# One order per engine for the whole of a hybrid encoder layer, with twenty-five instructions in other places

## The chip, the cores and the metric

The kernel runs on one core of a Trainium2 chip, in one launch. Its time is what the device takes for one execution, in microseconds (us); of a kernel run several times the median is given. The engines of the core are TensorE (PE in the profile: matmuls; PEld is its loading of weights), VectorE (DVE), ScalarE (ACT) and GpSimd (POOL); nearly all transfers are issued by SyncE (SP). Each engine takes its instructions one after the other in the order of the program, and waits at one whose inputs, or whose space for the output, are not ready.

## What is computed

One layer of an encoder, on 1024 rows of a new stream (the prompt) and 64 rows of a running one (the sample rows), 1024 wide:

```
z = x @ w_in, cut by columns into
  fox  (6 heads of 64): softmax(q k^T / 8 + c_t - c_s, causal) v,  c = cumsum(log f)
  sgu  (4 groups of 64): gelu(u) * (tril(w_s) @ layer_norm(gelu(v)) + b_s), chunks of 128
  sb   (6 heads of 64): stick-breaking weights in log space, strictly causal, times v
o = RMSNorm per head(concat) * g_mix
x = layer_norm(ALPHA * x + o @ w_out)
x = layer_norm(ALPHA * x + square(relu(x @ w_up)) @ w_down)       # 1024 -> 4096 -> 1024
```

The sample rows attend to 512 cached keys of their own as well. New keys, values and gates are outputs too. Everything is float32.

## The kernel before

A matmul of float32 accuracy is made from three passes in TensorE's faster format. Each operand is split into a high part, which ScalarE copies, and the rest, which VectorE or GpSimd subtracts (`split`, the subtraction is L182 throughout). So a tile that TensorE multiplies always comes from a pair of instructions on two engines.

**Attention** goes through three head pairs of fox and then three of stick-breaking. For each, keys and values of all rows are projected (L452, from `wkv` splits at L428), queries are projected, doubled by an exchange through a transfer (`qd`, L206, L602), and scores are made by blocks (`S`, L651). For fox VectorE takes maxima (`T` and `m`, L623), ScalarE exponentials; for stick-breaking VectorE scans (`sn`, L635). The weights are transposed on TensorE (`pt`, L699), split (`pth`, L667 and L182), multiplied with the values (`o`, L709 to L712), copied out (`osb`, L722), transposed again (`otp`, L730) and reduced (`ot`, L731). Beside the attention the output weights are brought in, scaled and put back to memory in parts (`rwo`, `swo`, `wo_dr`: L1074, L1081, L1082, L1085), and the spatial gate is computed. The output projection (`mx`, L335) and the layer norm follow.

**The border to the MLP** transposes the normed rows (L1293) and builds seven operand tiles `xo` per half of the rows by additions (L1313 to L1327) and splits (L1298, L1303, L182).

**The MLP** uses seven products for each two-by-two block (a Strassen scheme). Up (L1419, sixteen pairs `p`, each for two halves `s` of the rows of 288 and 256): the products go into PSUM banks `zA`, `zB`, `zC`, `zD`; ScalarE copies a zA into `sn` or `hh` (L1430), VectorE combines (L1433 to L1439), squares the positive part (L1451), makes sums (L1460 to L1463), and the result `hh` is stored to memory (`h_dr`, `h4_dr`, `h3_dr`, and `hs_dr` for the sample rows). Down (L1884, sixteen `g`, each with two `x`): rows `hx`, `awa`, `hr` of h are loaded and split, by way of a staging tile `st` in PSUM: ScalarE copies the high part (L1578), writes it to `st` (L1582), VectorE subtracts `st` from the rows (L1583). The weights `rd` are loaded (L1533), combined in place (L1551) and split (ScalarE L1357, then L182): tiles `wd` and `b12`. The products land in banks `A`, `B`, `D` and are added by VectorE to `acc` and, for the first tile, `awa` (L1849, L1851). A second layer norm ends the kernel (L1894, L1953 to L1997).

`st` takes its PSUM bank in turn from two, and one of these is the bank that `zD` of the first half uses as well.

**What sets the order.** The program is traced by a Python loop. From the start of attention to its end, four tables of letters and counts in `ORDER` fix the order of TensorE, ScalarE, VectorE and GpSimd: each instruction falls into a lane by the name of its output, each letter takes the next of a lane. After attention a scheduler places the instructions by its own costs, except inside blocks `with in_order(border)`, which tie each engine's instructions to the order in which the code writes them. SyncE has no table.

The diff touches `in_order`, two places in the function that traces the layer, and the tables.

## Time and profile before

| | us |
|---|---|
| median of three runs | 1377.58 |
| lowest and highest | 1376.11, 1380.68 |
| the profiled execution | 1378.24 |
| its span | 1376.2 |
| TensorE busy in it | 1317.1 |
| VectorE busy | 996.0 |
| ScalarE busy | 719.7 |
| GpSimd busy | 617.1 |

The mean granted clock of TensorE was 0.99. In the timeline a row has the start, the length of the busy time, the engine, the line, the operation, the output and its inputs by the program's names with the buffer numbers left out, the shapes, and a count where several alike were joined. What stands in brackets is the idle time of the engine ahead of the row and what ended it. In the table by stage each engine has its busy time, in the order PE, PEld, DVE, ACT, POOL, then the granted clock, the share of time that the transfer engines were busy, and GB/s.

### The profile page before, as it was taken

The numbers are of one execution on the slowest core, as the hardware profiler recorded it, in microseconds if no ns is written. First come the engines' busy times: TensorE is split into PE (matmuls) and PEld (weight loads), VectorE is DVE, ScalarE is ACT, GpSimd is POOL, SyncE is SP. The second block draws the span as 40 slices with busy tenths as digits, with TensorE's granted clock in tenths as the row PEclk, the third lists the DMA queues.
The fourth block names the chain that finished last, engine by engine and source line by source line (L and its number), as shares of the span: only waits on it lengthen the run. The fifth ranks groups of instructions, "written<-read, shape, count | busy, mean of one in ns | idle before, by whom it ended". The sixth has DMA issues, their size and how long they took to land.

```text
span 1376.2 us, 24318 instructions
## 1 busy us (share of the span) xinstructions
PE 1317.1 (96%) x8827; PEld 1200.1 (87%) x8827; DVE 996.0 (72%) x1797; ACT 719.7 (52%) x1561; POOL 617.1 (45%) x666
## 2 busy tenths in 40 slices
PE   7999999999989998999999999999999999999996
PEld 7898989999888997778899999999976787887774
DVE  4577666576888389678875877877677676767677
ACT  4366566566656376334523322322267676767665
POOL 3222222255675456657402221221176665655557
PEclk9999999999999999999999999999999999999999
DMA  7445565141303257432244435344567344434343
GB/s 227 108 118 143 163 189 145 52 100 43 103 13 76 63 185 252 140 115 70 77 153 135 144 119 171 131 131 162 176 219 277 123 146 142 142 119 159 99 136 131
DMA packets 158048, 185.64 MB, mean 135 GB/s; under 512 B 27740, under 2 KB 116124, under 8 KB 157928
## 3 DMA queue, kind: packets, MB, share of 16 engines
q1 hardware_dynamic: 155832, 183.01, 41.7%
q8 instruction: 70, 1.15, 0.4%
q10 hardware_dynamic: 2096, 1.07, 0.3%
q14 instruction: 50, 0.41, 0.1%
HBM read 117.65 MB, written 60.10 MB: 129 GB/s over the span
## 4 chain that ended last, share of the span: by engine, by line
PE 56%; DVE 14%; DMA 10%; ACT 8%; POOL 7%; issue 5%; SPq 0%; ACTq 0%; DVEq 0%; POOLq 0%
PE zA L1419 9%; PE zD L1419 6%; PE mx L335 5%; PE kvsb L452 5%; PE A L1884 5%; PE kvfox L452 3%; PE zB L1419 3%; DMA rwo<-w_out 3%; PE zC L1419 3%; DMA rd<-w_down 2%; PE D L1884 2%; POOL wd L182 2%; PE qsb L593 2%; DVE snsb L635 1%; POOL rd L1551 1%
## 5 line engine op out<-in xcount | busy, mean ns | idle before, releaser
L182 POOL TENSOR_TENSOR wa<-wr,wa 128x512 fp32r<-128x512 f32 x41 | 64.4, 1598 | 220.1 <-ACT wa L1357 202.5
L182 POOL TENSOR_TENSOR wd<-rd,wd 128x512 fp32r<-128x512 f32 x77 | 100.5, 1317 | 108.8 <-ACT wd L1357 104.3
L335 PE MATMUL mx<-xT,oTb 128*128 128x512 f32 (+1 forms) x416 | 105.1, 404 | 1.4 <-DVE oTb L182 1.3
L1419 PE MATMUL zD<-xo,ws 128*128 128x288 f32 (+1 forms) x720 | 97.5, 289 | 2.7 <-DVE h4a L1583 1.7
L1419 PE MATMUL zA<-xo,ws 128*128 128x288 f32 (+1 forms) x720 | 97.0, 289 | 0.0
L1419 PEld LDWEIGHTS zD<-xo,ws 128*128 128x128 f32 x720 | 93.4, 189 | 3.4 <-DVE h4a L1583 2.0
L335 PEld LDWEIGHTS mx<-xT,oTb 128*128 128x128 f32 (+1 forms) x416 | 76.0, 188 | 20.4 <-DVE oTb L182 2.2
L1551 POOL TENSOR_TENSOR rd<-rd 128x512 f32<-128x512 f32 x56 | 79.5, 1419 | 31.1 <-DVE b L182 28.8
L1419 PEld LDWEIGHTS zA<-xo,ws 128*128 128x128 f32 x720 | 93.4, 189 | 0.0
L452 PE MATMUL kvfox<-wkvfox,xT 128*128 128x256 f32 (+3 forms) x624 | 89.7, 292 | 3.1 <-ACT wkvfox L428 3.0
L452 PE MATMUL kvsb<-wkvsb,xT 128*128 128x256 f32 (+1 forms) x624 | 88.8, 287 | 0.4 <-ACT wkvsb L428 0.4
L637 POOL TENSOR_TENSOR sgsb<-sgsb,snsb 128x127 f32<-128x127 f32 (+7 forms) x48 | 59.6, 1244 | 65.9 <-DVE snsb L635 54.5
L1357 ACT ACTIVATE wd<-rd 128x512 fp32r<-128x512 f32 x105 | 63.5, 623 | 46.6 <-POOL rd L1551 23.6
L1884 PE MATMUL A<-wd,wd 128*128 128x512 f32 x312 | 83.4, 396 | 3.3 <-DVE acc L1851 2.3
L452 PEld LDWEIGHTS kvfox<-wkvfox,xT 128*128 128x128 f32 (+1 forms) x624 | 81.1, 191 | 4.4 <-ACT wkvfox L428 3.4
L635 DVE TENSOR_TENSOR_SCAN snsb<-snsb,one 128x128 f32<-128x128 f32 (+7 forms) x48 | 72.1, 1505 | 12.0 <-ACT snsb L634 10.9
L452 PEld LDWEIGHTS kvsb<-wkvsb,xT 128*128 128x128 f32 (+1 forms) x624 | 79.5, 187 | 0.8 <-ACT wkvsb L428 0.6
L1430 ACT ACTIVATE sn<-zA 128x256 f32<-128x256 f32 (+1 forms) x80 | 31.0, 390 | 85.2 <-PE zA L1419 74.9
L1884 PEld LDWEIGHTS A<-wd,wd 128*128 128x128 f32 x312 | 58.0, 188 | 19.5 <-DVE acc L1851 4.0
L1884 PE MATMUL A<-wd,h4a 128*128 128x512 f32 x240 | 64.5, 394 | 1.6 <-DVE awa L1851 0.8
L1640 ACT ACTIVATE ws<-wr 128x1024 fp32r<-128x1024 f32 x28 | 29.1, 1057 | 59.2 <-DVE wr L1369 59.2
L1884 PEld LDWEIGHTS A<-wd,h4a 128*128 128x128 f32 x240 | 44.6, 188 | 13.3 <-DVE awa L1851 1.2
(551 smaller groups left out, 3749.1 us busy)
## 6 DMA issues: line engine op xcount, KB each, us to landing
h_dr<-hh SPq DMA_DIRECT2D x30, 512.0 KB, 3.2
rd<-w_down SPq DMA_DIRECT2D x30, 512.0 KB, 4.5
wr<-w_up SPq DMA_DIRECT2D x13, 1024.0 KB, 5.5
hr<-h_dr SPq DMA_DIRECT2D x31, 384.0 KB, 4.4
h_dr<-hh SPq DMA_DIRECT2D x30, 384.0 KB, 3.6
raw<-w_in SPq DMA_DIRECT2D x44, 256.0 KB, 3.3
wo_dr<-swo SPq DMA_DIRECT2D x32, 256.0 KB, 2.3
xT<-wo_dr SPq DMA_DIRECT2D x8, 1024.0 KB, 7.0
```

Of the source, the lines that this page charges most:

```text
L182: eng.tensor_tensor(out, src, hi.bitcast(F32), op=ALU.subtract)
L335: nc.tensor.matmul(acc[0:m], oT[:, k, hx, 0:m], wo[k // 4][hw][:, k % 4, cs], start=(i == 0), stop=(i == len(seq) - 1))
L452: nc.tensor.matmul(acc[0:n, c0:c0 + n1 - n0], xT[k // 4][:, k % 4, c:c + n], wt[:, k, hw, n0:n1], start=(i == 0), stop=(i == len(seq) - 1))
L593: nc.tensor.matmul(acc[:, 0:w], wq[:, k, hw, :], xT[k // 4][:, k % 4, c:c + w], start=(i == 0), stop=(i == len(seq) - 1))
L635: nc.vector.tensor_tensor_scan(g[:, 0:n][:, ::-1], g[:, 0:n][:, ::-1], one.broadcast_to([P, n]), 1.0, op0=ALU.mult, op1=ALU.bypass)
L637: nc.gpsimd.tensor_tensor(s[:, 0:n - 1], s[:, 0:n - 1], g[:, 1:n], op=ALU.mult)
L1357: nc.scalar.activation(hi, raw, AF.Copy)
L1419: nc.tensor.matmul(z, w[:, hw, k], xop(s, bo, hx)[:, k, :], start=(new and k == 0 and j == 0), stop=(k == 3 and j == 2), skip_group_check= ...
L1430: nc.scalar.activation(c, z, AF.Copy)
L1551: eng.tensor_tensor(r[:, o], r[:, x], r[:, y], op=ALU.subtract)
L1640: nc.scalar.activation(ws[:, 0, q, c], src[:, q], AF.Copy)
L1884: nc.tensor.matmul(z, h[:, hx, q, o], wset[self.c % 2][q][:, hw, wb], start=((n in (0, 3) or n == 1 and self.c == 0) and q == 0 and j == 0 ...
```

## The change

The tables now hold numbers, one table an engine, and cover everything from the start of attention to the end of the program, MLP and border included. A word `n+k` means: n times, take the k-th of the instructions of this engine that are left, counted in the order of the trace. The order is laid down at the end of the trace, after everything has been written. `in_order` now ties SyncE's instructions alone, and the one use of it that was for TensorE alone is gone.

```diff
 ORDER = {}
-TICK = {"PE": {"kv": 0, "pt": 2, "sgm": 2, "mx": 1}, "ACT": {}, "DVE": {"T": 0, "sgvv": 0, "y": 0}, "POOL": {}}
-KIND = {
...
-}
 ORDER["PE"] = """
-8u e 8u 23e 24e' 8u k 8u k 14e 4u 2e' 10e 22e' 4u 8e k 4e 7u k 5u 12e 4u 14e' 2u 10e' 8e k 15e k e 14u 24e'
...
+9 8+23 55 +8 8+25 +8 14 4+34 2+10 45 4+1 7+13 1 +12 4+36 12 4+24 14 2+36 19 15+1 8 8+24 24 +8 8 8+1 9 8+1
...
     @contextmanager
-    def in_order(prev=None, only=None):
+    def in_order(prev=None):
...
         for i in traced[at:]:
-            if only is not None and i.engine != only:
+            if i.engine != nc.sync.engine:
                 continue
...
-        phase_1 = len(traced)
+        from_here = len(traced)
...
-        def lane_of(i, eng, code):
...
-        for eng, e in (("PE", nc.tensor), ("ACT", nc.scalar), ("DVE", nc.vector), ("POOL", nc.gpsimd)):
...
-            assert not any(lanes.values()), eng
-
...
-                    with in_order(border, nc.tensor.engine) if p == 2 else nullcontext():
+                    with nullcontext():
                         ch.product(i)
...
+    for eng, e in (("PE", nc.tensor), ("ACT", nc.scalar), ("DVE", nc.vector), ("POOL", nc.gpsimd)):
+        left = [i for i in traced[from_here:] if i.engine == e.engine]
+        prev = None
+        for word in ORDER[eng].split():
+            n, k = (int(x or d) for x, d in zip(re.match(r"(\d*)\+?(\d*)", word).groups(), (1, 0)))
+            for _ in range(n):
+                i = left.pop(k)
+                if prev is not None:
+                    tc.add_manual_dep(i, prev.name, mybir.DependencyInfo(
+                        mybir.DependencyClass.NoSync, mybir.DependencyReason.DATA), reason="order")
+                prev = i
+        assert not left, eng
```

Every engine has the same instructions as before. TensorE has them in the same order. On ScalarE and VectorE a dozen each stand elsewhere, on GpSimd one (L1953 of the sample rows' norm, now ahead of L1986), and on SyncE five places differ (in fox0 `raw2182_0` and `raw2182_1`, loads at L427, each pass a store of `swo7_0`; a load of cached keys, a load of `y4` and a load of `hr1_1` are the others). Line numbers are larger after the change: L1357, L1430, L1435, L1551, L1578, L1583 and L1851 become L1367, L1440, L1445, L1561, L1588, L1593 and L1861.

In attention: on VectorE `swo3_1` (L1082) goes behind `Tfox1_5_1` (L623), `swo7_0` behind `Tfox0_3_1`, `pthsb0_1_0_0` ahead of the second `qdsb0_3`, `otsb1_0_0` (L731) ahead of the scan of `snsb1_3_1`; on ScalarE `wqsb0` ahead of `Tfox0_3_0`, `osbfox0_0_0` ahead of `swo7_0`, `pthfox0_1_1_0` ahead of `swo7_1`, `qssb0` behind `osbsb0_0_1` and `pthsb0_1_0_1`. At the border to the MLP: on ScalarE one copy `xo13` goes behind `c123` (L1309) and one copy `xo14` ahead of `sn0_1` (L1430); on VectorE `hh1_0<-zD` goes ahead of `hh1_0<-zB`. The others lie at the border from up to down, at the start of the down products and in the last of them.

The first place is the border from up to down, where the last up products (`p` 15, half 0) meet the first splits for down. ScalarE before:

```order
L1430 ACTIVATE sn15_0_12435<-zA15_0_12437 128x288
L1357 ACTIVATE wd0_0_12451<-rd0_0_12254 128x512
L1357 ACTIVATE wd0_1_12452<-awa_12332 128x512
L1578 ACTIVATE h4a_12327<-h4a_12327 128x512
L1582 ACTIVATE st3_12472<-h4a_12327 128x512
```

ScalarE with the change:

```order
L1367 ACTIVATE wd0_0_12451<-rd0_0_12254 128x512
L1367 ACTIVATE wd0_1_12452<-awa_12332 128x512
L1588 ACTIVATE h4a_12327<-h4a_12327 128x512
L1440 ACTIVATE sn15_0_12435<-zA15_0_12437 128x288
L1592 ACTIVATE st3_12472<-h4a_12327 128x512
```

The copy of the product zA into `sn15_0` now comes after two weight copies and one copy of h. VectorE at the same place, before:

```order
L1435 TENSOR_TENSOR hh15_0_12436<-zB15_0_12457,sn15_0_12435 128x288
L1583 TENSOR_TENSOR h4a_12327<-h4a_12327,st3_12472 128x512
L1583 TENSOR_TENSOR h4a_12327<-h4a_12327,st4_12476 128x512
L1551 TENSOR_TENSOR rd0_0_12254<-rd0_0_12254 128x512
L1551 TENSOR_TENSOR awa_12332<-awa_12332 128x512
```

VectorE with the change:

```order
L1593 TENSOR_TENSOR h4a_12327<-h4a_12327,st3_12472 128x512
L1593 TENSOR_TENSOR h4a_12327<-h4a_12327,st4_12476 128x512
L1561 TENSOR_TENSOR rd0_0_12254<-rd0_0_12254 128x512
L1445 TENSOR_TENSOR hh15_0_12436<-zB15_0_12457,sn15_0_12435 128x288
L1561 TENSOR_TENSOR awa_12332<-awa_12332 128x512
```

The combination `hh15_0` of the product zB has moved behind both subtractions of h and one combination of weights. `st3` shares its bank with `zD15_0`.

Near the start of the down products VectorE moves three more: `wd0_1` by `st8` (L1583) goes behind the addition of `A0_0` to `awa`, and the addition of `A1_1` to `acc37` goes ahead of `h4b` by `st19` (L1583) and of the addition of `p11_1` to the same `acc37`. ScalarE takes one copy of `hr0_1` into `wd0_1` (L1578) before two weight copies (L1357).

The second place is in the last products, on ScalarE, ahead of the rows for the down product 13 (`hr13`, `hx`, `awa` are rows of h, `b12_0` is a weight tile made from `rd7_0`). Before:

```order
L1582 ACTIVATE st108_14998<-h4a_12327 128x512
L1578 ACTIVATE h4a_12327<-hx_12333 128x512
L1578 ACTIVATE h4a_12327<-awa_12332 128x512
L1578 ACTIVATE wd0_0_12451<-hr13_0_14899 128x384
L1578 ACTIVATE wd0_0_12451<-hr13_1_14901 128x384
L1357 ACTIVATE b12_0_12584<-rd7_0_14840 128x512
```

With the change:

```order
L1592 ACTIVATE st108_14998<-h4a_12327 128x512
L1367 ACTIVATE b12_0_12584<-rd7_0_14840 128x512
L1588 ACTIVATE h4a_12327<-hx_12333 128x512
L1588 ACTIVATE wd0_0_12451<-hr13_0_14899 128x384
L1588 ACTIVATE wd0_0_12451<-hr13_1_14901 128x384
L1588 ACTIVATE h4a_12327<-awa_12332 128x512
```

The weight copy `b12_0` has moved from behind four copies of h to ahead of them, and the copy from `awa` behind those from `hr13`. VectorE's addition of `ds6_1` (the sample rows' product) to `awa` goes ahead of one subtraction at the same time. A little earlier ScalarE takes a copy of `wd1_0` behind `st103`, `hr12_1` and the preload `B12_1` (L1872).

The third place is some fifteen microseconds later in the profile, on VectorE. Before:

```order
L1583 TENSOR_TENSOR h4b_12587<-awa_12332,st116_15169 128x512
L1851 TENSOR_TENSOR acc37_12748<-p113_1_15058,B13_1_15078 128x512
L182 TENSOR_TENSOR b12_1_12586<-rd7_1_15037,b12_1_12586 128x512
L1851 TENSOR_TENSOR acc26_12592<-acc26_12592,D13_0_15128 128x512
L1851 TENSOR_TENSOR acc37_12748<-acc37_12748,A13_1_15049 128x512
```

With the change:

```order
L1593 TENSOR_TENSOR h4b_12587<-awa_12332,st116_15169 128x512
L1861 TENSOR_TENSOR acc37_12748<-p113_1_15058,B13_1_15078 128x512
L1861 TENSOR_TENSOR acc26_12592<-acc26_12592,D13_0_15128 128x512
L215 TENSOR_TENSOR b12_1_12586<-rd7_1_15037,b12_1_12586 128x512
L1861 TENSOR_TENSOR acc37_12748<-acc37_12748,A13_1_15049 128x512
```

The addition of `D13_0` has passed the split of `b12_1`.

More of the change, by code (lines that the diff above doesn't have):

```diff
@@ L49 @@
 ORDER = {}
-TICK = {"PE": {"kv": 0, "pt": 2, "sgm": 2, "mx": 1}, "ACT": {}, "DVE": {"T": 0, "sgvv": 0, "y": 0}, "POOL": {}}
-KIND = {
-    "PE": "a:S b:Ss0 c:Ss1 d:ftp e:kv f:mx g:o h:op i:os j:otp k:pk l:pkc m:pt n:ptn o:pts p:q q:sgm "
-           "r:sgu s:sgv t:wstp u:xtp",
-    "ACT": "a:T b:f c:g d:gsv e:kc f:kn g:kp h:kvs i:oTb j:osb k:pth l:pths m:ptnn n:qd o:qs p:qsz "
-           "q:rawf r:sg s:sn t:so u:sq v:swo w:up x:vh y:wkv z:wq A:wst B:wu C:wv D:xT E:y",
-    "DVE": "a:S b:T c:car d:cum e:f f:fx g:g h:gsv i:kc j:kn k:kp l:kvs m:lf n:lsta o:lsum p:oTb q:oo "
-           "r:ot s:ots t:pth u:pths v:ptnn w:qd x:qs y:rge z:sgst A:sgvv B:sn C:ss D:swo E:up F:wkv G:wq "
-           "H:wst I:xT J:y",
-    "POOL": "a:cum b:lsta c:oo d:qsz e:rge f:sg g:sgst h:sguu i:sgvv j:ss k:vc l:vl m:vn n:vp o:wkv p:wq "
-           "q:wsr r:wu s:wv t:y",
-}
@@ L1242, in _build @@
                         flush()
-        def lane_of(i, eng, code):
-            nm = i.outs[0].bass_ap.tensor.name
-            m = re.match(r"([a-zA-Z]+\d?)_?(?:fox|sb)\d(.*)", nm) or re.match(r"([a-zA-Z]+)(.*)", nm)
-            nums, at = re.findall(r"\d+", m[2]), TICK[eng].get(m[1])
-            return code[m[1]] + ("'" if at is not None and at < len(nums) and int(nums[at]) % 2 else "")
-        for eng, e in (("PE", nc.tensor), ("ACT", nc.scalar), ("DVE", nc.vector), ("POOL", nc.gpsimd)):
-            code = dict(w.split(":")[::-1] for w in KIND[eng].split())
-            lanes = {}
-            for i in traced[phase_1:]:
-                if i.engine == e.engine:
-                    lanes.setdefault(lane_of(i, eng, code), []).append(i)
-            prev = None
-            for word in ORDER[eng].split():
-                n, k = re.match(r"(\d*)(.*)", word).groups()
-                for _ in range(int(n or 1)):
-                    i = lanes[k].pop(0)
-                    if prev is not None:
-                        tc.add_manual_dep(i, prev.name, mybir.DependencyInfo(
-                            mybir.DependencyClass.NoSync, mybir.DependencyReason.DATA), reason="order")
-                    prev = i
-            assert not any(lanes.values()), eng
     xst = ExitStack()
```

59 lines of the change are left out of this document (removed), and 104 rows, old and new, of the table ORDER.

## The prediction

> **What bounds the kernel now.** I read the page's busy times first, then the busy time of each engine by stage, then TensorE's rows with a bracket (idle time before the row, and who ended it), and last the rows of whoever is named there.
>
> ```profile
> PE 1317.1 (96%) x8827; PEld 1200.1 (87%) x8827; DVE 996.0 (72%) x1797; ACT 719.7 (52%) x1561; POOL 617.1 (45%) x666
> 0.00:672.00 672.00, 635.52 (x4695) 594.30 (x4696) 478.07 (x980) 373.70 (x894) 307.21 (x420) 0.98 0.41 120
> 672.00:702.00 30.00, 28.02 (x215) 26.56 (x214) 27.19 (x47) 12.10 (x24) 7.38 (x6) 1.00 0.33 113
> 702.00:997.00 295.00, 295.00 (x2346) 295.00 (x2346) 212.61 (x324) 81.91 (x155) 64.45 (x41) 1.00 0.44 147
> 997.00:1055.00 58.00, 51.68 (x261) 42.02 (x261) 46.42 (x67) 36.84 (x73) 42.08 (x32) 1.00 0.76 265
> ...
> 1285.00:1366.00 81.00, 76.83 (x322) 58.41 (x320) 59.84 (x118) 56.20 (x104) 51.43 (x49) 1.00 0.33 111
> 1366.00:1376.20 10.20, 0.00 (x0) 0.00 (x0) 6.44 (x12) 3.06 (x5) 4.19 (x8) 0.72 0.62 229
> ```
>
> The first number of a stage is its length, the second what TensorE was busy in it. TensorE is the bound: 1317.1 of 1376.2. The up products (702 to 997) have no hole at all, so no reordering there can gain anything. TensorE's holes are 36.5 us in attention and mixer, 2.0 at the border to the MLP, 6.3 at the border from up to down, 4.2 in the last products, and 10.2 after its last matmul. The change leaves TensorE's own order as it was: all it can do is let the other three release TensorE earlier or later at these holes. So I go through the holes that a moved instruction touches, and ask of each how much of it is the moved instruction's doing.
>
> **Border up to down (997 to 1055), the largest term.**
>
> ```profile
> 1000.99 0.41 ACT L1430 ACTIVATE sn<-zA 128x288 f32<-128x288 f32 x1 [1.71 <-PE zA L1419]
> ...
> 1004.75 0.46 DVE L1435 TENSOR_TENSOR hh<-zB,sn 128x288 f32<-128x288 f32 x1 [4.09 <-DMA hs_dr<-hh]
> 1005.13 1.27 DVE L1583 TENSOR_TENSOR h4a<-h4a,st 128x512 fp32r<-128x512 f32 x2
> ...
> 1005.86 1.85 PE L1419 MATMUL zD<-xo,ws 128*128 128x288 f32 x12 [1.74 <-DVE h4a L1583]
> ...
> 1006.32 0.91 DVE L1551 TENSOR_TENSOR rd<-rd 128x512 f32<-128x512 f32 x1
> ...
> 1006.65 1.74 POOL L182 TENSOR_TENSOR wd<-awa,wd 128x512 fp32r<-128x512 f32 x1
> 1007.16 1.77 DVE L1551 TENSOR_TENSOR awa<-awa 128x512 f32<-128x512 f32 x1
> ...
> 1008.86 1.78 DVE L1551 TENSOR_TENSOR rd<-rd 128x512 f32<-128x512 f32 x1
> ...
> 1011.06 1.86 PE L1419 MATMUL zD<-xo,ws 128*128 128x288 f32 x12 [0.18 <-DVE hh L1433]
> ...
> 1012.61 0.68 DVE L1551 TENSOR_TENSOR rd<-rd 128x512 f32<-128x512 f32 x1
> ```
>
> The PSUM bank that zD15_0 needs is held by the staging tile st3, until VectorE's subtraction at L1583 has read it. That subtraction stands behind hh15_0<-zB, which waits for the stores of the tile's earlier contents: VectorE idles 4.09, and TensorE 1.74. In the new order both subtractions and one L1551 stand ahead of hh15_0<-zB. ScalarE also does two wd copies and an h4a copy in the 1.71 it idled before sn15_0, so that st3 now comes right behind sn15_0, which ends at 1001.40. TensorE is ready at 1005.86 - 1.74 = 1004.12: that leaves 2.72 for one copy and one subtraction (half of 1.27), and the whole hole goes, **-1.74**. What is late next is the second zD, which waits for hh<-zD behind two more L1551. hh15_0<-zB still starts at 1004.75, and the row at 1011.06 comes after it by 6.31 with three L1551 between; with one of them taken out ahead, the first of 0.91 (some 0.84 from start to start) and the two subtractions (1.19 from 1005.13 to 1006.32) fall away from this chain, which so ends at 1009.0, against 1011.06 - 0.18 - 1.74 = 1009.14 at which TensorE is there. So its 0.18 goes too: **-1.92** together. The other end: if the first L1551, now ahead, also takes 1.78 instead of 0.91, hh15_0<-zB is pushed back by up to 0.87 and the second zD waits by about as much; then the border gives 1.05. I take -1.92, since the row of that first L1551 itself reads 0.91.
>
> L1551 takes 0.68 when VectorE has SBUF to itself and 1.78 beside a running POOL subtraction (1.74): each seems to wait for the other. [...]
>
> **Start of the down products.**
>
> ```profile
> 1024.96 0.96 PE L1884 MATMUL A<-wd 128*128 128x512 f32 x3 [0.68 <-DVE awa L1849]
> ...
> 1046.25 0.96 PE L1884 MATMUL A<-wd 128*128 128x512 f32 x3 [1.11 <-DVE acc L1849]
> ...
> 1051.34 0.68 DVE L1849 SCALAR_TENSOR_TENSOR acc<-acc,p 128x512 f32<-128x512 f32 x1
> ...
> 1052.67 0.97 PE L1884 MATMUL A<-wd,wd 128*128 128x512 f32 x3 [0.74 <-DVE acc L1849]
> ```
>
> At 1024.96 a subtraction (wd0_1 by st8) is moved behind the awa accumulation that TensorE waits for. It is only postponed: it now stands ahead of the accumulation that the next product of the other half waits for. I take -0.1 of the 0.68 (bounds 0 and -0.68). At 1052.67 the accumulation acc37<-A1_1 passes a subtraction at L1583 and the accumulation of 0.68, so it comes some 1.2 earlier (two starts of 0.6): the 0.74 goes. At 1046.25 the wait is for a loaded residual and not for the order; it gains only what its load is issued earlier: -0.15 (bounds 0 and -0.2). Together **-1.0**.
>
> **The last products.**
>
> ```profile
> 1287.07 1.19 PE L1884 MATMUL B<-wd,h4a 128*128 128x512 f32 x4 [0.30 <-ACT B L1872]
> ...
> 1296.02 0.63 ACT L1578 ACTIVATE h4a<-hx 128x512 fp32r<-128x512 f32 x1 [3.59 <-DMA hx<-h_dr]
> ...
> 1301.09 0.69 DVE L182 TENSOR_TENSOR b<-rd,b 128x512 fp32r<-128x512 f32 x1 [5.71 <-ACT b L1357]
> ...
> 1302.90 1.66 PE L1884 MATMUL A<-wd,h4a 128*128 128x512 f32 x6 [0.80 <-DVE awa L1851]
> ...
> 1304.75 0.96 PE L1884 MATMUL B<-wd,h4b 128*128 128x512 f32 x3 [0.19 <-ACT B L1872]
> ...
> 1314.48 1.38 DVE L182 TENSOR_TENSOR b<-rd,b 128x512 fp32r<-128x512 f32 x1 [1.49 <-ACT b L1357]
> ...
> 1315.78 0.67 DVE L1851 TENSOR_TENSOR acc<-acc,D 128x512 f32<-128x512 f32 x1
> ...
> 1317.10 0.96 PE L1884 MATMUL A<-wd,wd 128*128 128x512 f32 x3 [1.01 <-DVE acc L1851]
> ```
>
> At 1287.07 ScalarE's preload of B12_1 stood behind a weight copy that was late; the copy now stands behind it: -0.30. Near 1301 VectorE idles 5.71 for ScalarE's copy b12_0, which stood behind h4a<-hx and that one's 3.59 wait for a load. In the new order b12_0 goes first, into those 3.59; VectorE's split and the accumulation of awa, freed of it, are done long before 1302.90: -0.80, and the 0.19 at 1304.75, at the end of the same chain, too. At 1317.10 TensorE waits for an accumulation behind the b12_1 split (1.38, itself 1.49 late) and acc<-D (0.67). The change puts acc<-D ahead of the split, into its 1.49. That alone takes one start of 0.60 off; the full 1.01 goes only if the split too comes earlier, which hangs on a load. Between 0.60 and 1.01 I take 0.80. Together **-2.1**. After TensorE's last matmul nothing but a POOL operation of the sample rows moves; the 10.2 there stay.
>
> **Attention and the border to the MLP.**
>
> ```profile
> 164.47 0.75 DVE L1082 SCALAR_TENSOR_TENSOR swo<-rwo,gmx,swo 128x512 fp32r<-128x512 f32 x1 [1.89 <-ACT swo L1081]
> 165.14 0.68 DVE L623 CUSTOM_DVE_ANT_0 Tfox<-Sfox,cbfox 128x512 f32<-128x512 f32 x1
> ...
> 189.25 1.12 PE L651 MATMUL Sfox<-kpfox,qdfox 128*128 128x256 f32 x4 [2.47 <-DVE mfox L623]
> ...
> 302.00 0.38 PE L709 MATMUL osb<-pthsb,vpsb 128*128 128x256 f32 x1 [0.77 <-ACT osbsb L722]
> ...
> 376.69 0.42 DVE L731 TENSOR_REDUCE otsb<-otpsb 128x128 f32<-128x256 f32 x1
> ...
> 377.26 0.41 PE L730 MATMUL otpsb<-ident,osbsb 128*128 128x128 f32 x2 [1.72 <-DVE otsb L731]
> ...
> 676.32 1.85 PE L1419 MATMUL zC<-xo,w 128*128 128x288 f32 x12 [0.43 <-ACT c L1309]
> ...
> 683.50 1.14 ACT L1303 ACTIVATE xo<-xr 128x512 fp32r<-128x512 f32 x2
> ...
> 701.79 0.94 PE L1419 MATMUL zD<-xo,ws 128*128 128x288 f32 x5 [0.77 <-DVE hh L1433]
> ```
>
> At 164.47 the maximum of Tfox1_5_1 (0.68) goes into VectorE's idle 1.89 instead of behind it. What follows on VectorE is up to 0.68 earlier, down to the large hole at 189.25: 0 to -0.68, and I take -0.6, as nothing else in that stretch idles VectorE so long. The holes at 302.00 and 377.26 go only in part, since several releases end close together there. At 302.00 osbsb passes qssb, but the transpose that comes next needs VectorE's otsb as before: I take a third of 0.77. At 377.26 otsb's 0.42 leaves the chain ahead of the next pthsb, and no more than that is won; the next wait for VectorE takes some back: -0.3. In all **-1.15**, with bounds 0 and -3.2 (0.68 and both holes whole).
>
> At the border to the MLP a copy xo13 leaves ScalarE's path to c: -0.43. The first product of VectorE's two at 701.79 is the one that TensorE waits for, now ahead of the other (some 0.4). But a copy xo14 (half of 1.14) now stands ahead of sn0_1, which frees the bank of TensorE's next zA: +0.57. Net **-0.2**, between -0.8 and +0.6.
>
> **The sum.** -1.92 - 1.0 - 2.1 - 1.15 - 0.2 = -6.4. The profiled execution took 1378.24, its span 1376.2; 2.04 lie outside the span, which the change doesn't touch. 1378.24 - 6.4 = 1371.9. The median of the runs is 1377.58, 0.66 under the profiled one, so I expect a median near **1371.2**. With the low bounds (-1.05, -0.74, -1.7, 0, +0.6) the sum is -2.9, with the high ones (-1.92, -1.6, -2.3, -3.2, -0.8) it is -9.8.
>
> **The rivals.**
>
> [...] At the border L1551 takes 1.78 wherever it stands, and the second zD waits 0.87: the sum is -5.5, the time 1372.1. For it: two of the first three L1551 rows read 1.77 and 1.78. Against it: POOL, released earlier too, may be through before.
>
> *Each hole closed opens the next.* TensorE arrives sooner at the next wait, whose releaser has not moved: a load, or an engine that is just as full. Then only the places with a long idle time behind them keep their gain: 1.74 at 1005.86 and 0.80 at 1302.90, -2.5 in all, 1375.1. For it: attention has 36.5 us of holes, most of which nothing moved touches. Against it: behind 1005.86 and after 1055 TensorE runs without holes over long stretches, so a gain there has nothing to be given back to.
>
> *Nothing comes of it.* The releases named in brackets are inferred; if others ended the waits, TensorE's unchanged order keeps its time: 1377.6.
>
> *Slower, by SP's queue.* In the middle of fox0 the load raw2182_0 is moved ahead of a store of swo7_0.
>
> ```profile
> 223.24 2.55 POOL L182 TENSOR_TENSOR wqsb<-raw,wqsb 128x512 fp32r<-128x512 f32 x2 [10.19 <-ACT wqsb L428]
> ...
> 225.71 0.39 SPq L427 DMA_DIRECT2D raw<-w_in  x1
> ```
>
> The load overwrites what POOL's two subtractions read, so it waits for the first of them (ends about 224.5). Behind it on SP now stand both stores, the next weight load and the query exchange qdfox0_3, for which TensorE's next scores wait. As POOL ends now, over a microsecond is left to 225.71. It decides once POOL is later than that: every microsecond more is one for TensorE. Were POOL to idle its 10.19 again behind ScalarE, SP would be about 9 late, and the time 1371.2 + 9 = 1380. Against it: in the new order ScalarE's wqsb copy, which POOL waits for, comes one place earlier.
>
> **How the numbers follow.** Forecast 0.57 (1368 to 1373.4), port 0.14, next hole 0.18, nothing 0.06, SP's queue 0.05. A measurement of this kernel can tell 0.3% from no change, 4.1 us: faster means below 1373.45. The forecast and the port count as faster, but for a twentieth, and a fifth of the next-hole case: 0.71. Slower by over 0.3% is part of SP's case and what I haven't seen: 0.05. The rest, 0.24, is the same. The range of 8 in 10 reaches from 1367.8 (the high bounds leave 1367.8) to 1376.2, so that the next-hole case is in it.
>
> **What would show it.** Right: the rows of TensorE that were at 1005.86, 1052.67, 1302.90 and 1317.10 stand without a bracket or with one under 0.3; TensorE's holes are 3.5 to 4.5 in the stage 997 to 1055 instead of 6.3, about 2 instead of 4.2 in the last one; the stage of up products still has none; the tail is still 10.2. The port: an L1551 of 1.78 ahead of hh15_0<-zB, and a bracket of 0.5 or more at the second zD. The next hole: the named brackets gone, but new ones within some ten microseconds of them. SP: raw at the head of SP's queue with POOL as releaser, and a bracket from qdfox at TensorE. I am wrong altogether if TensorE's rows at those places keep their brackets, or if its holes in attention grow by over 3.

## The result, and the profile after

The change takes 1366.41 us (median of 6 runs, 1363.60 to 1367.45), the kernel before beside it 1377.53 (6 runs, 1376.11 to 1380.68). The ratio is 0.9913, interval 0.9900 to 0.9925: **11.1 us faster**, where 6.4 were forecast, and 1.4 under the range. Measured twice more, on two chips, the ratio was 0.9942 (0.9922 to 0.9961) and 0.9921 (0.9891 to 0.9951). So the gain is 8 to 11 us. The 6.4 lies under all three, though the interval of the second still holds it.

Busy times and stages of the changed kernel; in a stage row stand the length, then busy time of TensorE, its weight loads, VectorE, ScalarE and GpSimd, the granted clock, the transfer engines' share and GB/s:

```profile
PE 1312.3 (96%) x8827; PEld 1197.7 (88%) x8827; DVE 996.5 (73%) x1797; ACT 719.8 (53%) x1561; POOL 618.2 (45%) x666
...
693.80:988.00 294.20, 294.20 (x2338) 294.20 (x2339) 213.93 (x324) 81.39 (x153) 64.80 (x41) 1.00 0.44 146
988.00:1045.00 57.00, 53.71 (x272) 44.73 (x271) 45.85 (x66) 37.81 (x75) 41.82 (x32) 0.97 0.78 272
...
1274.00:1351.30 77.30, 75.91 (x324) 59.07 (x322) 57.89 (x114) 54.25 (x100) 51.38 (x48) 1.00 0.32 111
1351.30:1361.80 10.50, 0.00 (x0) 0.00 (x0) 6.73 (x13) 3.08 (x5) 4.39 (x9) 0.66 0.63 233
```

The up products still have no hole, and from TensorE's last matmul to the end are 10.5, as before (the 10.2 that the prediction names is the length of a window that opens 0.3 after the last matmul). TensorE's holes (length less busy) fell from 6.3 to 3.3 around the border from up to down, and from 4.2 (of which 0.3 are that piece of the tail) to 1.4 in the last products.

The border in the timeline of the change:

```profile
993.91 0.69 DVE L1593 TENSOR_TENSOR h4a<-h4a,st 128x512 fp32r<-128x512 f32 x1 [1.26 <-ACT st L1592]
...
995.69 1.85 POOL L215 TENSOR_TENSOR wd<-rd,wd 128x512 fp32r<-128x512 f32 x1 [1.25 <-ACT wd L1367]
995.70 0.68 DVE L1561 TENSOR_TENSOR rd<-rd 128x512 f32<-128x512 f32 x1
995.95 1.75 PE L1429 MATMUL zD<-xo,ws 128*128 128x288 f32 x12
...
998.01 1.77 DVE L1561 TENSOR_TENSOR rd<-rd 128x512 f32<-128x512 f32 x1
...
1000.71 1.75 PE L1429 MATMUL zD<-xo,ws 128*128 128x288 f32 x12
```

Both zD rows, 1005.86 and 1011.06 before, stand without a bracket. The moved L1551, which is L1561 here, took 0.68, and GpSimd's subtraction, issued at the same moment, 1.85, against 1.29 for each of the two before it; the next L1561 on `rd` took 1.77. In this pairing it is GpSimd that took longer, so a 0.68 can stand beside a running subtraction too, and TensorE has no bracket from GpSimd in this stage. With the L1561 of 1.77 both were long: it stands beside subtractions of 1.74 from 997.51 and from 999.20. At the moved L1561 it was the same in all eleven traces with the new order: 0.68 or 0.69 and 1.85 or 1.86. In the three with the old order that first L1551 took 0.91, 1.50 and 1.79.

The start of the down products, with the stages behind its largest hole:

```profile
1022.46 0.73 PE L1894 MATMUL A<-wd,h4b 128*128 128x512 f32 x2 [1.77 <-ACT h4b L1588]
1023.64 1.22 PE L1894 MATMUL A<-wd,h4a 128*128 128x512 f32 x2 [0.45 <-ACT h4a L1588]
...
1022.00:1024.00 2.00, 1.09 (x3) 0.66 (x4) 0.93 (x2) 1.94 (x4) 1.86 (x4) 0.91 0.60 242
1024.00:1026.00 2.00, 2.00 (x6) 1.52 (x6) 1.93 (x6) 1.97 (x5) 0.60 (x1) 0.50 0.75 286
1026.00:1028.00 2.00, 2.00 (x8) 1.63 (x7) 2.00 (x4) 2.00 (x5) 1.92 (x2) 0.74 1.01 338
```

The brackets at 1052.67 (0.74), 1046.25 and 1024.96 are gone, but TensorE, earlier now, waits 1.77 for a high part of ScalarE's, and behind it the granted clock falls to half for 3.41 us, from 1023.64 on. That was not forecast; more of it below.

Last products, then attention and the border to the MLP:

```profile
1290.64 1.53 PE L1894 MATMUL A<-wd,h4a 128*128 128x512 f32 x6
...
1346.81 1.66 PE L1894 MATMUL A<-wd,wd 128*128 128x512 f32 x6 [0.96 <-DVE acc L1861]
```

```profile
185.28 0.38 PE L684 MATMUL Sfox<-kpfox,qdfox 128*128 128x256 f32 x1 [1.60 <-DVE mfox L656]
...
370.88 0.33 PE L763 MATMUL otpsb<-ident,osbsb 128*128 128x128 f32 x1 [0.77 <-ACT osbsb L755]
372.02 0.39 PE L744 MATMUL osb<-pthsb,vpsb 128*128 128x256 f32 x1 [0.46 <-DVE pthsb L215]
...
390.34 0.39 PE L485 MATMUL sgv<-wv,xT 128*128 128x256 f32 x1 [1.72 <-DVE sgvv L884]
...
676.54 0.62 PE L1429 MATMUL zA<-xo,oTb 128*128 128x256 f32 x3 [0.25 <-ACT sn L1440]
...
693.78 0.40 PE L1429 MATMUL zD<-xo,ws 128*128 128x288 f32 x1 [0.32 <-DVE hh L1443]
```

From 1270 on TensorE had six brackets (3.6 in all) and has one, the 0.96 near its end, which was 0.99 before. In attention 2.47 became 1.60; 1.72 became 0.77 and a new 0.46 right behind it; the wait for sgvv (1.71 before, 1.72 now) was nobody's aim and stays.

Both profiles together, by length: from the start of one matmul to the start of the same later one, both named by their time in the profile of before (the first stage from the start of the span).

| | 0–163 | 163–545 | 545–665 | 665–712 | 712–960 | 960–1065 | 1065–1270 | 1270–1352 |
|---|---|---|---|---|---|---|---|---|
| before | 163.0 | 382.05 | 120.0 | 46.92 | 248.13 | 105.08 | 205.00 | 81.94 |
| change | 160.6 | 378.63 | 118.7 | 46.09 | 248.13 | 102.74 | 205.00 | 77.90 |
| less | 2.4 | 3.4 | 1.3 | 0.83 | 0 | 2.34 | 0 | 4.04 |

The two long stages without moved instructions and without holes agree to 10 ns. But 0–163 has no moved instruction either, and is 2.4 shorter. So this pair of executions can't be read as the change alone: the experiments have to say how such a length scatters.

### The profile page after: what moved, and what is told of

Read it like the earlier page. It is cut to its first block, busy times and chain, and to the rows that moved or that the text cites. A ratio compares the mean times of both kernels' runs of the same rounds, so it can differ in the third digit from the quotient of the medians.

```text
span 1361.8 us, 24315 instructions
## 1 busy us (share of the span) xinstructions
PE 1312.3 (96%) x8827; PEld 1197.7 (88%) x8827; DVE 996.5 (73%) x1797; ACT 719.8 (53%) x1561; POOL 618.2 (45%) x666
## 3 DMA queue, kind: packets, MB, share of 16 engines
q8 instruction: 70, 1.15, 0.4%
## 4 chain that ended last, share of the span: by engine, by line
PE 71%; DVE 12%; DMA 5%; ACT 4%; POOL 4%; issue 3%; SPq 0%; ACTq 0%; DVEq 0%; POOLq 0%
PE A L1894 11%; PE zA L1429 9%; PE zD L1429 6%; PE mx L368 5%; PE D L1894 5%; PE kvsb L485 5%; PE kvfox L485 3%; PE zC L1429 3%; PE zB L1429 3%; PE B L1894 3%; PE qfox L626 2%; DMA rwo<-w_out 2%; DVE snsb L668 2%; DMA raw<-w_in 2%; PE Sfox L684 1%
## 5 line engine op out<-in xcount | busy, mean ns | idle before, releaser
L1561 POOL TENSOR_TENSOR rd<-rd 128x512 f32<-128x512 f32 x56 | 79.5, 1420 | 24.8 <-DVE b L215 22.5
L1367 ACT ACTIVATE wd<-rd 128x512 fp32r<-128x512 f32 x105 | 63.4, 623 | 41.4 <-POOL rd L1561 20.9
L1440 ACT ACTIVATE sn<-zA 128x256 f32<-128x256 f32 (+1 forms) x80 | 30.9, 389 | 83.8 <-PE zA L1429 67.6
L1861 DVE TENSOR_TENSOR acc<-acc,A 128x512 f32<-128x512 f32 x73 | 49.1, 680 | 9.0 <-PE A L1894 8.9
```

The costliest lines, as they stand in the source:

```text
L1367: nc.scalar.activation(hi, raw, AF.Copy)
L1440: nc.scalar.activation(c, z, AF.Copy)
L1561: eng.tensor_tensor(r[:, o], r[:, x], r[:, y], op=ALU.subtract)
L1861: nc.vector.tensor_tensor(out, out if other is None else other, bank, op=ALU.add)
```

## The experiments

Kernels measured together share a chip and the runs of before. A group of moves is undone by giving instructions of one engine their former places in the finished order: at such a position, so many instructions in this permutation. By these lists 23 instructions of these engines moved (twelve on ScalarE, ten on VectorE, one on GpSimd), not the 24 or 25 named elsewhere. The kernels with such a list have line numbers a few higher than the change. All compute the whole layer.

### Each group undone alone

Theory A: a hole costs its bracket, a short refill behind it and sometimes a stretch at half clock, so each group is worth what its stage lost between the two profiles. Theory B: the terms of the sum were right, and what came beyond them is scatter.

```diff
+    "ACT": ((1024, (3, 0, 1, 2)), (1041, (1, 2, 3, 4, 5, 6, 7, 8, 9, 10, 0)),),
+    "DVE": ((1270, (3, 0, 1, 2)), (1287, (5, 0, 1, 2, 3, 4)), (1324, (1, 2, 0)),),
```

> The changed kernel, with the five moves between 997 and 1055 (the border from up to down, and the start of the down products) put back to the old order; the other nineteen places stay changed. Theory A (each hole of TensorE costs its bracket, a short refill behind it and, after some, a stretch at half clock; read from the shift between the two traces, which grows by 2.35 us in this stage): 1366.4 + 2.35 = 1368.8, a ratio to before of 0.9937. Theory B (the terms of my sum were right, and what came beyond them is scatter between executions): 1366.4 + 2.9 = 1369.3, 0.9940. Both expect the brackets of 1.7 and 0.7 at zD and at acc<-A1_1 to be back.

```diff
+    "ACT": ((1403, (3, 0, 1, 2)), (1417, (1, 4, 2, 3, 0)), (1470, (1, 0)),),
+    "DVE": ((1601, (1, 0)), (1619, (1, 0)),),
+    "POOL": ((623, (1, 0)),),
```

> The changed kernel, with the six places in the last products and the tail (b12_0, wd1_0, ds6_1, D13_0, one h copy, the POOL operation of the sample rows) put back. Theory A: the traces differ by 4.05 us here (brackets 2.5, the rest refill), so 1366.4 + 4.05 = 1370.4, ratio 0.9949. Theory B: 1366.4 + 2.1 = 1368.5, ratio 0.9935.

```diff
+    "ACT": ((262, (1, 0)), (265, (1, 0)), (276, (1, 0)), (370, (2, 0, 1)),),
+    "DVE": ((222, (1, 0)), (309, (1, 0)), (414, (1, 0)), (503, (1, 2, 0)),),
```

> The changed kernel, with the eight moves in attention put back (SyncE's order follows). Theory A: the traces differ by 2.96 us between 165 and 547, of it 1.05 in a stretch at half clock behind the hole of 2.47 at 189, and by 1.34 more in a stretch at half clock near 549: 1366.4 + 3 to 4.3 = 1369.4 to 1370.7, ratio 0.994 to 0.995, with the half-clock stretch near 189 back in the trace. Theory B: 1366.4 + 1.15 = 1367.6, ratio 0.9928, and the clock near 189 has nothing to do with the moves.

```diff
+    "ACT": ((844, (2, 0, 1)), (854, (1, 0)),),
+    "DVE": ((940, (1, 0)),),
```

> The changed kernel, with the three moves at the border to the MLP (copies xo13 and xo14 on ScalarE, the two hh1_0 additions on VectorE) put back. Theory A: the traces differ by 0.82 us there: 1367.2, ratio 0.9925. Theory B: 0.2: 1366.6, ratio 0.9921. The two are hardly to be told apart by time; the trace has to show the brackets of 0.43 and 0.77 back.

| undone | us | ratio to before (interval) |
|---|---|---|
| border and start of down | 1369.19 | 0.9956 (0.9938–0.9974) |
| last products | 1369.80 | 0.9956 (0.9937–0.9975) |
| attention | 1369.75 | 0.9958 (0.9939–0.9977) |
| border to the MLP | 1367.65 | 0.9936 (0.9915–0.9957) |

The change itself was not run beside these four, and the intervals are about ±2.5 us wide, too wide for terms of 1 to 3. So the times don't decide between the two theories; the rows and stage lengths tell more. TensorE's rows where a group is undone, from the border, the last products, attention (two) and the border to the MLP:

```profile
1000.62 0.67 PE L1433 MATMUL zD<-xo,ws 128*128 128x288 f32 x3 [2.11 <-DVE h4a L1597]
```

```profile
1296.86 0.50 PE L1899 MATMUL A<-wd,h4a 128*128 128x512 f32 x1 [0.83 <-DVE awa L1866]
```

```profile
186.31 0.38 PE L688 MATMUL Sfox<-kpfox,qdfox 128*128 128x256 f32 x1 [2.23 <-DVE mfox L660]
...
374.11 0.41 PE L767 MATMUL otpsb<-ident,osbsb 128*128 128x128 f32 x2 [1.73 <-DVE otsb L768]
```

```profile
699.08 1.59 PE L1433 MATMUL zD<-xo,ws 128*128 128x288 f32 x10 [0.78 <-DVE hh L1447]
```

These are the brackets of before (1.74, 0.80, 2.47, 1.72, 0.77), each back at its place with its releaser. So the moved groups are what ended these waits, as the prediction read it. The half clock near 189, which theory A wanted back with attention undone, did not come back.

### The old order in the new code, and the change again

All four groups undone at once, which gives every engine the order of before:

> The changed kernel's code with all twenty-four places put back: the instruction order of the kernel before, on every engine, laid down in the new way. It is a second look at the kernel before. Theory A1 (what the trace of before lost ahead of 165, where nothing is moved, and at half clock near 189 and 549 is an accident of that one execution; the moves give their brackets and a refill behind each): time as before, ratio 0.998 to 1.002, but a profile that stands 1 to 3 us earlier at 165 than the first trace of before. Theory A2 (the stretches at half clock belong to the old order, since its holes are longer): time as before, and the stretches near 189 and 549 there again, with the same shift of 0 at 165.

> The changed kernel once more, beside the others of this call, for a time from the same chip and a second trace. Theory A1: ratio 0.991 to 0.994 and stage by stage, against the old order's second trace: 0.8 less at the border to the MLP, 1.5 to 2.5 less from 997 to 1070, 3 to 4 less from 1285 on, 0.3 to 1.2 less in attention. Theory A2: the same, but 2.5 to 4 less in attention.

1374.43 us, ratio 0.9997 (0.9982 to 1.0012): the way the order is laid down costs and gains nothing; the gain is in the moves. The change again gave 1368.20 beside it, ratio 0.9942. The stage lengths of these profiles, and of three kernels that follow below (bold: the stage's group in the old order; in brackets: partly so, or with further moves):

| | 0–163 | 163–545 | 545–665 | 665–712 | 960–1065 | 1270–1352 |
|---|---|---|---|---|---|---|
| before | 163.0 | **382.05** | 120.0 | **46.92** | **105.08** | **81.94** |
| old order, new code | 160.3 | **382.06** | 119.9 | **46.95** | **105.09** | **79.20** |
| border undone | 161.3 | 380.81 | 118.2 | 46.12 | **105.65** | 78.05 |
| end undone | 162.2 | 378.93 | 120.4 | 47.61 | 102.80 | **81.14** |
| attention undone | 161.0 | **380.12** | 118.7 | 46.11 | 103.35 | 77.97 |
| MLP border undone | 162.4 | 380.61 | 119.3 | **46.93** | 103.48 | 77.93 |
| change | 160.6 | 378.63 | 118.7 | 46.09 | 102.74 | 77.90 |
| change again | 160.9 | 377.92 | 119.7 | 46.12 | 102.30 | 78.12 |
| change, third time | 160.2 | 378.28 | 119.8 | 46.12 | 102.68 | 77.93 |
| copy xo14 undone | 160.5 | 380.01 | 118.6 | (46.08) | 103.61 | 77.93 |
| subtraction by st8 undone | 163.5 | 380.35 | 119.4 | 47.59 | (102.48) | 78.16 |
| four further moves | 160.4 | (379.07) | 121.2 | 46.08 | 102.51 | 79.84 |

Old against new by the means of these rows, those in brackets left out: border 105.3 to 102.9, **-2.3** (forecast -2.9); end 80.8 to 78.2, **-2.6** (-2.1); border to the MLP 46.93 to 46.11 without the two odd ones, in which TensorE waited 1.08 for xr at a place that nothing moved touches, **-0.8** (-0.2); attention 381.4 to 379.4, **-2.0** (-1.15), with a scatter of ±1.5. Together -7.7. The first and the third column hold no instruction that any of these kernels moves, and run from 160.2 to 163.5 and from 118.2 to 121.2 all the same.

Against the old order's second profile the change again took 0.8 less at the border to the MLP, 2.8 at the border, 1.1 at the end and 4.1 in attention. Theory A1 had named 0.8, 1.5 to 2.5, 3 to 4 and 0.3 to 1.2, so one pair of profiles misses in three of four stages.

One order doesn't even leave the same holes. The end in the old order, once more, VectorE's split first and then TensorE:

```profile
1295.16 0.69 DVE L220 TENSOR_TENSOR b<-rd,b 128x512 fp32r<-128x512 f32 x1 [4.97 <-ACT b L1372]
...
1298.09 1.53 PE L1899 MATMUL A<-wd,h4a 128*128 128x512 f32 x6
```

The row at 1298.09 is the one that had 0.80 before and 0.83 with the end undone; here it has nothing. VectorE's split, which waits for ScalarE's copy, starts 2.9 ahead of it, where before it was 1.8 (1301.09 to 1302.90). A bracket read from one execution is one draw.

### The copy xo14

The only term that spoke against the change was xo14 ahead of sn0_1, +0.57. That move undone alone:

```diff
+    "ACT": ((854, (1, 0)),),
```

> The changed kernel with the copy xo14 put back behind sn0_1 on ScalarE, the one move that I sized as a loss (+0.57). By my term the time falls by 0.5, and TensorE's bracket of 0.25 at zA0_1 (ScalarE's sn) goes. The rival: xo14 is waited for later in the same stage, by the product that reads it, and the 0.25 comes back there: no difference in the stage 672 to 702.

1368.66 us, ratio 0.9948 (0.9932 to 0.9965), so no gain by undoing it beside the change's 1368.20. The stage 665–712 took 46.08, as with the change (46.09 to 46.12). TensorE's rows from the first zA of the second half to zC, in the change and then with xo14 back:

```profile
673.39 1.54 PE L1429 MATMUL zA<-xo,w 128*128 128x256 f32 x12
...
676.54 1.64 PE L1429 MATMUL zA<-xo,oTb 128*128 128x256 f32 x12 [0.25 <-ACT sn L1440]
...
680.92 1.58 PE L1429 MATMUL zC<-xo,w 128*128 128x256 f32 x12
```

```profile
674.60 1.54 PE L1432 MATMUL zA<-xo,w 128*128 128x256 f32 x12
...
678.70 1.81 PE L1432 MATMUL zD<-xo,oTb 128*128 128x256 f32 x12
...
680.89 1.38 PE L1432 MATMUL zA<-xo,oTb 128*128 128x256 f32 x10 [0.15 <-DVE xo L218]
682.11 1.53 PE L1432 MATMUL zC<-xo,w 128*128 128x256 f32 x12
```

From 673.39 to 680.92 are 7.53, from 674.60 to 682.11 are 7.51 (and before, 681.02 to 688.54, 7.52). With the copy late, TensorE waits two products further on for the operand that the copy begins; with the copy early it waits for the bank. The two waits stand in for each other: the term was 0, not +0.57.

Right ahead of this, another wait did open. Where the hole of 0.43 for c is closed, TensorE's wait for xr some 2 us further on is 0.88 to 0.89 instead of 0.34, in every trace with this order; with the group undone both are back. The place of the hole for c became 1.00 shorter, which is more than its bracket and 0.25 and not taken apart further, and that of xr 0.53 longer, so 0.47 is left of it.

### Do the holes closed open others?

Two moves for which I had a doubt. First the subtraction that the change puts behind the awa accumulation at the start of down, back at its place:

```diff
+    "ACT": ((1041, (1, 2, 3, 4, 5, 6, 7, 8, 9, 10, 0)),),
+    "DVE": ((1287, (5, 0, 1, 2, 3, 4)),),
```

> The changed kernel with one pair of moves at the start of the down products put back: the copy and the subtraction of wd0_1 by st8, which I gave -0.1. In the traces with the move TensorE waits 0 to 1.8 near 1022 for ScalarE's copy h4b of rows awa that a transfer brings, which the traces of the old order don't show. If the move brings that about (awa's tile comes free later), putting it back takes up to 1.8 away and brings the 0.7 at A0_0 back: 0.3 to 1 less than the changed kernel. If the wait is the transfer's own scatter, it stays, and the time is 0.1 to 0.6 more.

1367.91 us, ratio 0.9937 (0.9916 to 0.9958); the stage 960–1065 took 102.47, inside the change's 102.30 to 102.74. The 1.77 ahead of 1022.46 was not there, but 0.54 for awa was back. At the matmul of 1022.46 the wait for h4b stands in eight of the ten traces with the move (0.4 to 1.8) and in none of the four without it, so the move seems to bring it about. By its stage the move is worth nothing here, near its -0.1. The time is 3.8 above the change's 1364.16 on the same chip, with intervals that overlap; the two stages that are long in its profile, 0–163 and 665–712, hold nothing that was undone.

Then four further moves of the same kind in attention, each ahead of a bracket that the change left:

```diff
+    "DVE": ((536, (1, 0)), (561, (2, 0, 1)), (596, (2, 0, 1)), (693, (2, 0, 1)),),
```

> The changed kernel with four more places of VectorE's order in attention moved, at brackets of TensorE that stand in every trace so far: sgvv3 (what TensorE waits for at 390) ahead of a multiplication of sgvv2, otsb1_2_0 (406) ahead of two operations of sgvv5, pthsb1_3_0_3 (432) ahead of a weight split and of g1v8, pthsb2_3_0_0 (524) ahead of g1u3 and a split of kc_sb. Theory C (only a bracket that recurs in every execution of an order can be taken out by order, and each taken out gives its length and a refill): brackets of 1.7, 0.5 to 1.4, 1.7 and 1.2, of which 1.5, 0.8, 1.4 and 1.2 go, 4.9 in all, at most 6 with refills: 3.5 to 6 less than the changed kernel in the same call, ratio to it 0.9956 to 0.9974. Theory D (in attention a hole closed opens the next, as the next-hole rival had it): under 1.5 less, with new brackets near 391, 407, 434 and 525.

> The changed kernel in the same call as the two above, to compare them with. Against the kernel before: ratio 0.991 to 0.995 by its two earlier measurements. In its trace the brackets at 185 (1.4 to 1.7), 390 (1.7) and 432 (1.7) stand as in the other traces of its order; stretches at half clock lie elsewhere than in the other two.

1370.26 us, ratio 0.9957 (0.9938 to 0.9976), beside the change's 1364.16, 0.9921 (0.9891 to 0.9951), on the same chip: 6.1 more, with intervals that barely overlap, where theory C had 3.5 to 6 less and theory D up to 1.5 less. The stage took 379.07, the change's traces 377.92 to 378.63, which is not all of the 6.1; where the rest comes from stays open. TensorE's rows:

```profile
394.81 0.38 PE L488 MATMUL sgv<-wv,xT 128*128 128x256 f32 x1 [0.87 <-DVE sgvv L887]
...
432.50 0.47 PE L934 MATMUL sgm<-vh,wst 128*128 128x256 f32 x2 [0.83 <-DVE qdsb L638]
```

The 1.72 for sgvv is halved, and at the stage's end nothing of it is left; one of the holes further on is 0.83 for qdsb. In attention, where VectorE is behind TensorE again and again, a closed hole need not be a gain.

### What one hole costs

The brackets closed came to less than the stages gained in the end (six brackets of 3.6 to one of 0.96 are 2.7, the stage lost 4.04). So I made holes where there are none, among the up products: there ScalarE's copy of the fifth product is done again several times over, so that VectorE's hh<-zD and TensorE behind it wait. Only the repeats are added.

```diff
...
+                if i == 4 and s == 0:
+                    before = [traced[-1]]
+                    for _ in range(DOSE.get(p, 0)):
+                        nc.scalar.activation(c, z, AF.Copy)
+                        again.append((traced[-1], before[0]))
...
```

Large holes first (14 to 27 repeats in six of the products), then short ones (5 to 13 in eleven):

> The changed kernel with holes of graded length made in the up products, where TensorE has none: in the pairs 3, 5, 7, 9, 11 and 13 ScalarE's copy hh<-zA of the fifth product (half 0) is repeated 14, 16, 18, 20, 23 and 27 more times (the result is the same), so that VectorE and then TensorE wait. A repeat costs about 0.3. From one trace, place by place: what TensorE is late by behind the hole, against the length of its bracket. If a hole costs its bracket alone, the two agree; by theory A the lateness is 0.15 to 0.35 more, and behind holes of over 2 to 2.5 us the granted clock falls to a half for some 3 us, which costs 1 to 1.5 more. With repeats of 0.3 and a slack of some 4 us the brackets should run from 0 to about 4.

> As the kernel with holes of graded length, with fewer repeats (5 to 13, one place in each of the pairs 3 to 13): brackets of 0.3 to 3.3. There every hole of 3.5 to 9.2 was followed by half clock and cost 1.75 to 2.7 beyond its bracket. Theory A: holes under 2 cost 0.15 to 0.35 beyond the bracket and leave the clock whole, those over 2.5 drop it. If the drop hangs on where the hole falls and not on its length alone, some of 1.5 to 3 drop it and others of the same length don't.

They took 1410.82 and 1380.90 us (one run each). What a hole costs beyond its bracket, by an example: TensorE in the kernel with short holes, and the same products in the change.

```profile
854.60 3.19 PE L1433 MATMUL zC<-xo,wa 128*128 128x288 f32 x24
860.09 3.30 PE L1433 MATMUL zD<-xo,ws 128*128 128x288 f32 x24 [2.30 <-DVE hh L1452]
863.24 3.19 PE L1433 MATMUL zA<-xo,wa 128*128 128x288 f32 x24
```

```profile
847.84 3.19 PE L1429 MATMUL zC<-xo,wa 128*128 128x288 f32 x24
850.86 3.19 PE L1429 MATMUL zD<-xo,ws 128*128 128x288 f32 x24
853.89 3.19 PE L1429 MATMUL zA<-xo,wa 128*128 128x288 f32 x24
```

From zC to zA are 8.64 there and 6.05 here: the hole cost 2.59 for a bracket of 2.30, 0.29 more. In the same way for the others (us):

| bracket | 0.52 | 0.79 | 0.97 | 0.98 | 1.42 | 1.86 | 1.86 | 2.30 | 3.51 | 3.63 | 4.51 | 5.40 | 6.73 | 9.21 |
|---|---|---|---|---|---|---|---|---|---|---|---|---|---|---|
| cost beyond it | 0.24 | 0.26 | 0.26 | 0.26 | 0.25 | 0.26 | 1.79 | 0.29 | 2.67 | 1.78 | 1.75 | 2.49 | 2.29 | 2.43 |

Two prices. Some **0.25 for every hole** (0.24 to 0.29 behind the brackets of 0.52 to 2.30 that kept the clock): so much TensorE lost as it stopped and started again. For the example it can be read off the rows above: in the change zC's row ends at 851.03, and zD's starts at 850.86, 0.17 before that end. These matmuls overlap so, and a bracket, which is counted from the end, leaves this out. The other 0.12 come behind the hole: from zD to zA are 3.15 there and 3.03 here. And 1.5 to 2.4 more behind some, where the granted clock was halved. Both brackets of 1.86, each with two windows of 3.41 us (after the length stands TensorE's busy time; the clock is the third number from the end; the last section says why these windows):

```profile
769.54 1.87 PE L1433 MATMUL zD<-xo,ws 128*128 128x288 f32 x10 [1.86 <-DVE hh L1452]
...
767.28:770.69 3.41, 1.55 (x12) 1.34 (x11) 1.48 (x4) 1.89 (x5) 0.00 (x0) 1.00 0.83 280
770.69:774.10 3.41, 3.41 (x18) 3.41 (x17) 2.14 (x2) 1.67 (x3) 2.30 (x2) 0.50 0.00 0
```

```profile
949.54 1.74 PE L1433 MATMUL zD<-xo,ws 128*128 128x288 f32 x11 [1.86 <-DVE hh L1452]
...
944.76:948.18 3.42, 2.92 (x24) 2.72 (x22) 0.00 (x0) 3.17 (x9) 0.00 (x0) 1.00 0.61 212
948.18:951.59 3.41, 2.05 (x15) 2.05 (x16) 1.61 (x5) 2.62 (x6) 1.72 (x2) 1.00 0.00 0
```

The same place in two pairs of products and the same bracket, but half clock behind the one and full clock behind the other. Every hole of 3.51 and more was followed by half clock.

The kernel's own holes have the first price too. Around five places (28 matmuls each; 16 at the last) the profile of before is longer than the change by 2.00 for the bracket of 1.74 at 1005.86, 0.44 for 0.18 at 1011.06, 0.59 for 0.30 at 1287.07, 1.54 for 0.80 and 0.19 at 1302.90, and 1.37 for 1.01 at 1317.10: 0.26 to 0.36 a hole.

With 0.25 a hole the end closes: 2.66 less in brackets and five holes fewer, 2.66 + 1.25 = 3.9 for the 4.04 of the table; and with the end undone, four holes and 2.39 more than the change, 3.4 for 3.0 to 3.2. At the border from up to down the change has 3.16 less in brackets and three holes fewer, 3.9, but its profile has the half clock around 1024, (1 - 0.91 + 1 - 0.50 + 1 - 0.74) x 2.00 = 1.7: 2.2 for the measured 2.34. In the other two profiles of the change the clock stayed at 1.00 there; the same account gives 3.1 and 3.0 for 2.8 and 2.4, so it is good to some 0.6.

## Why the prediction was right in kind and too small

**The bound and the mechanism held.** TensorE is the bound, its order is the same, and the gain lies at the holes whose releaser moved, with that releaser. The marks that were named are there: no bracket at the rows that were at 1005.86, 1052.67, 1302.90 and 1317.10, none in the up products, an unchanged tail. Holes around the border fell to 3.3, just under the 3.5 to 4.5 named, and in the last products to 1.4, under "about 2".

**The step that failed is the price of a hole.** Each term took a bracket for all that its hole costs. A hole costs its bracket and some 0.25 besides, in the made holes as in the kernel's own. Over the last three stages with moves, 18 brackets became 10: 8 x 0.25 = 2.0 that no term had.

**One term was not there.** xo14 at +0.57 was a wait ahead of a wait: TensorE would have stood two products later for the operand. Without it the border to the MLP is -0.43 - 0.4 = -0.83, and it measured -0.83. That the two agree to the last digit is luck: by places the stage is 1.00 and 0.47 shorter and 0.53 longer, and the 0.53, the wait for xr, was in no term.

With both, 6.4 + 2.0 + 0.6 = 9.0, against 7.6 to 11.1 by the medians of three comparisons, 9.9 in the mean, and 7.7 by the stages with moves. So the two steps are not the whole of the first result's 11.1: some 2 of it have no term, and by the second comparison's 7.6 the time would have lain within the range.

**The other terms.** The first zD was right, -1.74 whole. The second was right in the three profiles of the change, but not in every execution of its order, as the first rival below shows. The start of down was over-forecast in effect: its brackets went, but TensorE met a wait of 0.4 to 1.8 for h4b, which varies from one trace of the change to another, and one of 0.35 to 0.71 for the accumulation ahead of D, where the postponed subtraction now stands. At 1046.25 and behind it some of the old brackets are there again in the change's other two profiles. So -2.9 for the stage measured -2.3, with the refills in it. The last products were mis-sized by the refills, -2.1 against -2.6. For attention the three brackets fell by 0.87, 0.6 and 0.5, near 2.0 against the -1.15 taken: the -0.6, a third of 0.77 and -0.3 were too careful. The stage, with its ±1.5, says no more than that.

**The rivals.** The first, an L1551 of 1.78 wherever it stands (the port, 0.14), fell at the place where it was put: the L1561 that was moved took 0.68 or 0.69 in every trace of the new order. Behind it its sign is there: with the MLP border undone, and with the four further moves, hh15_0<-zB stood 0.78 and 0.89 for the store of hs_dr, the two operations of the moved kind behind it took 1.68 to 1.81, and the second zD had brackets of 0.67 and 0.59. That VectorE and GpSimd wait for each other in such rows was my reading of their lengths; no run shows a port, or what else the two would share. The next hole is true in part: in attention (four more moves won nothing), at the start of down, and at the border to the MLP, where the wait for xr grew. At the first zD and at the end it is not. That nothing would come of it fell with the rows that came back when a group was undone. SP's queue was half there; GpSimd's two subtractions, the load and the exchange on the queue, and SP's wait, in the change:

```profile
217.40 2.53 POOL L215 TENSOR_TENSOR wqsb<-raw,wqsb 128x512 fp32r<-128x512 f32 x2 [9.05 <-ACT wqsb L461]
...
218.71 0.37 SPq L460 DMA_DIRECT2D raw<-w_in  x1
...
222.62 1.60 SPq L239 DMA_DIRECT2D qdfox<-qdfox  x2
...
SPq L460 <- POOL wqsb L215: 1.2, 1, 1.2
```

GpSimd idled 9.05 behind ScalarE again, and the load waited 1.2 for its first subtraction, which was the first half of the sign. The second half is missing: TensorE has no bracket from qdfox from 210 to 240, so the exchange behind the load still came in time.

**The range** was made of sizes alone. It had no room for what an execution adds: single runs of before went from 1369 to 1386.

**What stays open.** Of the 14.4 between the first two spans some 4 lie in stages without a moved instruction. They are put down to the scatter that the table shows, and no run took them apart further. Whether the gain of an average execution is nearer to 8 or to 11 is not settled by three comparisons with intervals of ±2 to ±4.

## What to carry to other kernels

When TensorE is the bound, count a hole at its bracket plus what the restart costs (0.25 here), and look behind the longer ones for a lower granted clock (it came each time that TensorE was busy under 0.48 of a window of 3.41 us); many small holes are worth more than they look. A wait that a move adds costs only what TensorE wouldn't have stood for anyway a little later: follow the operands two products on before booking a loss, and likewise before booking a gain. And a stage's holes from one trace are one draw: where the same untouched stage differs by 2 to 3 us between traces, the range needs that much on each side.
